# Doubling the angles of the S5 recurrence once for all groups of states, and a new order of the streams, in a two-layer mixer trunk

## Chip, cores and metric

One Trainium2 chip, one core. The metric is the device time of one execution in microseconds: 1331.64 us is the median of three runs of the kernel before (1329.62 to 1334.2 us).

## What is computed

A trunk of two layers over 512 tokens of width 1024, batch 1, all in float32. Each layer is

```python
h = rmsnorm(x, g)
for each branch n of (a, b, c, d, e):
    o_n = branch_n(h @ w_in)            # 256 columns
    mixed += sigmoid(h @ w_gate_n) * ((silu(h @ w_z_n) * o_n) @ w_out_n)
x = x + mixed @ w_out
```

with a: differential attention (two softmaxes per head, four heads in two pairs), b: dilated attention, c: an S5 state space recurrence, d: attention over compressed, selected and window keys, e: attention over a memory of 256 rows. The recurrence has 16 groups of channels, each with 64 complex states. Its transition over one step is a magnitude and an angle per state; the kernel works in chunks of 8 tokens (TC = 8) of which there are 64 (NJ = 64), so it needs cosine and sine of 8, 16, 32, ..., 256 times the angle of each state.

## The kernel before

**Products.** Every weight comes in halves of 128x512, in all 408. Each is split in a high part (`whi`, a ScalarE copy) and a low part (`wlo`), and every product takes three matmuls: high by high, low by high, high by low (`acc<-hh,whi`, `acc<-hl,whi`, `acc<-hh,wlo`). The low part is made in one of two ways, which `weights_hi` chooses for each half: by a VectorE subtraction (`wlo<-raw,whi`, 136 halves), or by a ScalarE copy with factor -1 and a GpSimd DMA that adds the weight from memory again (`wlo<-wu`, line 296, 272 halves).

**Streams.** The program is written as Python generators ("streams"): projections (each branch's q, k, v and the like from h), attentions (three workers that take the heads one by one), compression of branch d, recurrences, memories, and the trunk (gates and merges of the branches, 40 merge steps per layer, and the output product). While the program is built, a model of the engines runs with it: the stream with the lowest rank whose wake time has passed issues next. `RANK` (line 42) gives the ranks, `AFTER` (line 41) the event after which the recurrences (`s`, `c`) and memories begin, `PA` (line 44) how many heads of the branch before may still be unfinished when the next projections of d and a start. What the chip gets is the order that comes out, per engine; all instructions carry line 244 (line 286 for DMAs of SyncE's queue), so a group in the profile is told by its tiles.

**Names of tiles.** `acc`: a product's sum in PSUM; `sc`: scores; `prob`: probabilities (a ring of NPROB = 3); `pt`, `ph`, `pl`: a transposed tile and its high and low part; `o`: a head's output; `gate`: a merge's gate; `bl`, `bh`: the parts of a gated branch; `cxh`: inputs of the compression, whose products are `ms<-whi,cxh`; `tmp`: scratch; `u`, `uc`, `m`, `r`, `e`, `p`, `c`, `cs`: tiles of the recurrence; `s`: scratch of its parameters; `da`, `db`, `ck`, `sk`: four columns of an angle's doubling.

**Recurrence.** `s5_params` (from line 605) computes the parameters of all states of both layers at once, on tiles 128x16 (a column per layer and group of groups): exponentials, sine and cosine, and three doublings to 8 times the angle. `s5_table` (line 1550) makes, for each layer and each half of the groups, the table of 64 cosines and sines in six steps: six GpSimd products per step, and on VectorE ten operations on 128x4 tiles that double the angle, with a correction of its length, for the next step. Five such batches of ten belong to each of the four tables. `s5_operators` calls it and then `s5_powers`; `s5_in` makes `u`, sends it through memory (`ud`, `uc`) and `s5_chunks` does products with the states and a scan along the chunks (`r`). The recurrence of layer 0 runs beside its a heads and merges, that of layer 1 likewise.

**Heads of a.** `head_a` (line 1106) takes two probability tiles, one per softmax, and combines them.

## Time and profile before

| | before |
|---|---|
| time, median of three runs | 1331.64 us (1329.62 to 1334.2) |
| profiled execution | 1330.57 us |
| its span, first to last instruction | 1328.8 us |
| granted TensorE clock, mean | 0.984 |
| TensorE busy | 1261.2 us, 95% |
| VectorE busy | 917.0 us, 69% |
| ScalarE busy | 835.2 us, 63% |
| GpSimd busy | 433.8 us, 33% |
| data moved by DMA | 224.75 MB |

The span is the time from the first to the last instruction on the core; some 1.8 us of the execution lie outside it. In the trace's rows the first number is the start in microseconds from the span's start, the second the duration; matmuls overlap, so that two of 512 columns that last 0.39 us each start 0.23 us apart. In brackets stands how long the engine had been idle, and whose result ended that. Engines are named PE (TensorE), DVE (VectorE), ACT (ScalarE), POOL (GpSimd), SP (SyncE).

### The profile page before, as it was taken

Reading aid. Unit: us, or ns where it says so; the run is one execution under the profiler, and the core shown is the slowest. Engines: PE = TensorE matmul, PEld = TensorE weight load, DVE = VectorE, ACT = ScalarE, POOL = GpSimd, SP = SyncE. Lnnn points to the kernel's source line nnn. Section 1 sums busy time; section 2 is a strip of 40 time slices with the busy share of each in tenths; the row PEclk is TensorE's granted clock in tenths of the full one; section 3 lists DMA queues with packets and bytes.
Section 4 is the critical chain, followed back from the end, with each engine's and each line's share of the span. In section 5 each row is a group of like instructions: output and inputs, shape, how many; then the busy total and the mean of one; then the engine's idle time right before and its main releaser. Section 6 shows DMA issues by size and latency. Waiting matters only on the chain.

```text
span 1328.8 us, 19737 instructions
## 1 busy us (share of the span) xinstructions
PE 1261.2 (95%) x6303; PEld 1036.2 (78%) x6303; DVE 917.0 (69%) x2281; ACT 835.2 (63%) x1682; POOL 433.8 (33%) x551
## 2 busy tenths in 40 slices
PE   7699899999999999999989899999999999999996
PEld 4578678888887778888878588888877887888885
DVE  6879889667888775445338778677898776634542
ACT  6587877777774564655547767677768654455542
POOL 2643432221354262221223352122246335222112
PEclk9799999999999999999999899999999999999998
DMA  8484886754987788797766786374787888788751
GB/s 270 108 188 109 185 208 156 165 142 103 191 193 160 191 191 193 169 218 192 214 167 139 176 204 148 105 159 111 169 179 158 197 175 178 174 176 185 185 171 64
DMA packets 135816, 224.75 MB, mean 169 GB/s; under 512 B 23072, under 2 KB 30368, under 8 KB 135712
## 3 DMA queue, kind: packets, MB, share of 16 engines
q0 software_dynamic: 46080, 83.91, 38.8%
q1 hardware_dynamic: 89632, 139.59, 33.2%
q8 instruction: 49, 0.80, 0.2%
q14 instruction: 55, 0.45, 0.1%
HBM read 199.82 MB, written 23.56 MB: 168 GB/s over the span
## 4 chain that ended last, share of the span: by engine, by line
PE 74%; DVE 14%; DMA 5%; issue 3%; ACT 2%; POOL 1%; SPq 0%; DVEq 0%; POOLq 0%; ACTq 0%
PE acc L244 61%; PE ms L244 3%; PE sc L244 3%; PE o L244 3%; PE pt L244 3%; DVE prob L244 2%; DVE tmp L244 1%; DVE rope L244 1%; DMA raw<-wu 1%; DMA wlo<-wu 1%; DVE gate L244 1%; DVE c L244 1%; DVE pl L244 1%; POOL c L244 1%; POOL wlo L296 1%
## 5 line engine op out<-in xcount | busy, mean ns | idle before, releaser
L244 PE MATMUL acc<-hh,whi 128*128 128x512 f32 x1136 | 459.3, 404 | 10.8 <-ACT whi L244 6.2
L244 PE MATMUL acc<-hl,whi 128*128 128x512 f32 x1136 | 447.2, 394 | 1.3 <-DVE hl L244 1.3
L244 PE MATMUL acc<-hh,wlo 128*128 128x512 f32 x1136 | 446.9, 393 | 1.3 <-DVE wlo L244 1.3
L296 POOL DMA_DIRECT2D wlo<-wu x272 | 243.7, 913 | 606.2 <-ACT wlo L244 525.9
L244 ACT CAST whi<-raw 128x512 fp32r<-128x512 f32 x408 | 251.1, 617 | 265.4 <-PE acc L244 225.7
L244 PEld LDWEIGHTS acc<-hh,whi 128*128 128x128 f32 x1136 | 215.6, 190 | 58.6 <-issue 7.0
L244 PEld LDWEIGHTS acc<-hh,wlo 128*128 128x128 f32 x1136 | 215.1, 189 | 49.2 <-DVE wlo L244 2.2
L244 PEld LDWEIGHTS acc<-hl,whi 128*128 128x128 f32 x1136 | 216.0, 190 | 40.1 <-DVE hl L244 2.8
L244 ACT ACTIVATE wlo<-raw 128x512 fp32r<-128x512 f32 x272 | 170.2, 626 | 12.7 <-DMA raw<-wu 8.9
L244 DVE TENSOR_TENSOR wlo<-raw,whi 128x512 fp32r<-128x512 f32 x136 | 94.2, 696 | 45.7 <-ACT whi L244 45.4
L244 ACT ACTIVATE prob<-prob,nb 128x256 f32<-128x256 f32 (+3 forms) x160 | 89.3, 559 | 13.8 <-DVE nb L244 13.0
L244 ACT CAST ph<-pt 128x512 fp32r<-128x512 f32 (+1 forms) x112 | 58.2, 524 | 56.3 <-PE pt L244 53.7
L296 POOL DMA_DIRECT2D mixed<-gate x48 | 45.0, 937 | 140.2 <-DVE gate L244 98.7
L244 DVE TENSOR_TENSOR gate<-acc,rep 128x512 f32<-128x512 f32 x80 | 55.0, 688 | 49.4 <-PE acc L244 49.2
L244 DVE CUSTOM_DVE_ANT_0 prob<-sc,cst 128x128 f32<-128x128 f32 (+3 forms) x128 | 60.8, 486 | 31.7 <-PE sc L244 31.1
L244 PE MATMUL acc<-mx,whi 128*128 128x512 f32 (+1 forms) x288 | 81.0, 367 | 0.0
L244 DVE TENSOR_TENSOR pl<-pt,ph 128x512 fp32r<-128x512 f32 (+1 forms) x112 | 67.5, 608 | 18.6 <-ACT ph L244 18.3
L244 DVE SCALAR_TENSOR_TENSOR gate<-gate,acc 128x512 f32<-128x512 f32 x80 | 54.8, 685 | 28.1 <-ACT gate L244 23.8
L244 ACT ACTIVATE gate<-gate,hb 128x512 f32<-128x512 f32 x80 | 57.7, 721 | 15.4 <-DVE gate L244 15.2
L244 PE MATMUL pt<-cst,prob 128*128 128x128 f32 x384 | 61.9, 275 | 2.7 <-DVE prob L244 2.6
L244 PE MATMUL acc<-bh,whi 128*128 128x512 f32 x160 | 63.3, 396 | 0.8 <-DVE gate L244 0.8
L244 PE MATMUL acc<-bl,whi 128*128 128x512 f32 x160 | 62.6, 392 | 1.0 <-DVE bl L244 1.0
(310 smaller groups left out, 2110.4 us busy)
## 6 DMA issues: line engine op xcount, KB each, us to landing
raw<-wu SPq DMA_DIRECT2D x408, 256.0 KB, 4.3
wlo<-wu POOLq DMA_DIRECT2D x272, 256.0 KB, 5.6
mixed<-gate POOLq DMA_DIRECT2D x48, 256.0 KB, 5.0
mixed<-gate SPq DMA_DIRECT2D x16, 256.0 KB, 4.8
gate<-mixed SPq DMA_DIRECT2D x16, 256.0 KB, 4.3
x<-xT SPq DMA_DIRECT2D x8, 256.0 KB, 5.8
tab<-rope SPq DMA_DIRECT2D x8, 256.0 KB, 6.5
mraw<-memT SPq DMA_DIRECT2D x8, 256.0 KB, 5.8
```

The lines of the kernel that those rows point to most:

```text
L244: getattr(self.eng, name)(out, *args, **kw)
L296: self.eng.dma_start(out, src, accum_op=ALU.add)
```

## The change

1. `s5_params` goes on doubling, from 8 to 256 times the angle, on its 128x16 tiles, and keeps the six cosines and sines. These are five more rounds of ten VectorE operations, once. `s5_table` reads them: its five batches of ten operations on 128x4 tiles, for each of four tables, are gone (200 VectorE operations less, 50 more). The GpSimd products stay.
2. `AFTER['s']` is `pb` in place of `mem`: the parameters may begin after layer 0's projections of b, not after the memories'.
3. The attentions' rank is 4, not 3.
4. `PA[1]` is 1, not 4: in layer 0 the projections of a's second pair wait until at most one head of the first pair is left.
5. `head_a` waits until fewer than NPROB - 1 = 2 others hold a pair of probability tiles.

```diff
--- before.py
+++ after.py
@@ -38,10 +38,10 @@
 LAT = 100
 ORDER = ('beda', 'edba')
 MERGES = ('bedac', 'edbac')
-AFTER = {'s': 'mem', 'c': ('mem', 'ob'), 'm': ('b', 'a')}
-RANK = {'att': 3, 'cmp': 1, 'rec': 2, 'ch': 6, 'proj': 4, 'trunk': 5, 'mem': 3}
+AFTER = {'s': 'pb', 'c': ('mem', 'ob'), 'm': ('b', 'a')}
+RANK = {'att': 4, 'cmp': 1, 'rec': 2, 'ch': 6, 'proj': 4, 'trunk': 5, 'mem': 3}
 WORKERS = 3
-PA = (4, 4, 2, 1)
+PA = (4, 1, 2, 1)
 MEM0 = ('rep', 0)
 
 MAGIC = 12582912.0
@@ -599,7 +599,7 @@
 
     C16 = 16
     s5p = {}
-    for n in ("mag8", "c8", "s8", "zr", "zi", "ar1", "ai1", "ar2", "ai2", "ar4", "ai4"):
+    for n in (*(f"{x}{TC << i}" for x in "cs" for i in range(6)), "mag8", "zr", "zi", "ar1", "ai1", "ar2", "ai2", "ar4", "ai4"):
         s5p[n] = cp.tile([128, C16], F32, name="s5" + n)
 
     def s5_params():
@@ -687,23 +687,28 @@
         v.tensor_mul(zi, zi, den)
 
         c, s, m = cs, sn, mag
-        for n in (2, 4, 8):
-            c2, s2, m2 = (s5p["c8"], s5p["s8"], s5p["mag8"]) if n == 8 else (t16("c"), t16("s"), t16("m"))
+        n = 1
+        while n < TC * NJ // 2:
+            n *= 2
+            c2, s2 = (s5p[f"c{n}"], s5p[f"s{n}"]) if n >= TC else (t16("c"), t16("s"))
             v.tensor_mul(c2, c, c)
             v.tensor_mul(t, s, s)
             v.tensor_sub(c2, c2, t)
             v.scalar_tensor_tensor(s2, c, 2.0, s, ALU.mult, ALU.mult)
-            v.tensor_mul(m2, m, m)
+            if n <= TC:
+                m2 = s5p["mag8"] if n == TC else t16("m")
+                v.tensor_mul(m2, m, m)
+                m = m2
             v.tensor_mul(t, c2, c2)
             v.tensor_mul(u, s2, s2)
             v.tensor_add(t, t, u)
             v.tensor_scalar(t, t, -0.5, 1.5, ALU.mult, ALU.add)
             v.tensor_mul(c2, c2, t)
             v.tensor_mul(s2, s2, t)
-            if n < 8:
+            if n < TC:
                 v.tensor_mul(s5p[f"ar{n}"], m2, c2)
                 v.tensor_mul(s5p[f"ai{n}"], m2, s2)
-            c, s, m = c2, s2, m2
+            c, s = c2, s2
         for eng, name, args in ops:
             getattr(eng, name)(*args)
             yield eng.now + 130
@@ -1089,7 +1094,7 @@
         R["pa", l, i] = st, vs
 
 
-    outs, left = {}, {}
+    outs, left, pairs = {}, {}, []
 
     def out_tile(key):
         if key not in outs:
@@ -1108,6 +1113,8 @@
         st, vs = R["pa", l, i]
         vv = [x.rearrange("p (t h c) -> p t h c", t=2, h=2) for x in vs]
         ps, ds = [], []
+        yield lambda: len(pairs) < NPROB - 1
+        pairs.append(0)
         for c in range(2):
             q, k = st["a_q", hh], st["a_k", hh]
 
@@ -1117,6 +1124,7 @@
             p, den = yield from causal_exp(qk, causal, SC32)
             ps.append(p)
             ds.append(den)
+        pairs.pop()
         free(st["a_q", hh], st["a_k", hh])
         r0, r1 = recip(ds[0], 4), recip(ds[1], 4)
         V.tensor_scalar(r1[:, :4], r1[:, :4], lam[l], None, ALU.mult)
@@ -1553,9 +1561,9 @@
         V.memset(ct[:, :, 0:1], 1.0)
         V.memset(st[:, :, 0:1], 0.0)
         o = 8 * l + 4 * h
-        ck, sk = s5p["c8"][:, o:o + 4], s5p["s8"][:, o:o + 4]
         n = 1
         while n < NJ:
+            ck, sk = s5p[f"c{TC * n}"][:, o:o + 4], s5p[f"s{TC * n}"][:, o:o + 4]
             x, y = (xy[:, 128 * i:128 * i + 128].rearrange("p (s t) -> p s t", s=4)[:, :, 0:n] for i in range(2))
             cb, sb = ck.unsqueeze(2).to_broadcast([128, 4, n]), sk.unsqueeze(2).to_broadcast([128, 4, n])
             c0, s0 = ct[:, :, 0:n], st[:, :, 0:n]
@@ -1568,19 +1576,6 @@
             G.tensor_tensor(y, c0, sb, ALU.mult)
             G.tensor_tensor(s1, x, y, ALU.add)
             n *= 2
-            if n < NJ:
-                a, b, c, s = small(4, "da"), small(4, "db"), small(4, "ck"), small(4, "sk")
-                V.tensor_mul(a, ck, ck)
-                V.tensor_mul(b, sk, sk)
-                V.tensor_sub(c, a, b)
-                V.scalar_tensor_tensor(s, ck, 2.0, sk, ALU.mult, ALU.mult)
-                V.tensor_mul(a, c, c)
-                V.tensor_mul(b, s, s)
-                V.tensor_add(a, a, b)
-                V.tensor_scalar(a, a, -0.5, 1.5, ALU.mult, ALU.add)
-                V.tensor_mul(c, c, a)
-                V.tensor_mul(s, s, a)
-                ck, sk = c, s
 
     def s5_powers(l, h, x, y, tmp, conj):
```

Edits 2 to 5 and the missing operations change the order that comes out. TensorE's instructions are the same ones. VectorE has 2119 in place of 2259, among them 146 low parts in place of 136; ScalarE makes 262 low parts in place of 272, and GpSimd issues as many accumulating DMAs fewer. Up to the 270th row of TensorE (about 79 us of the trace of before), from about 555 to 1005 us and from about 1195 us the orders of all engines are alike. Between, in layer 0, the value projections of d (dv) come after the compression, the projections of a's second pair move from among the merges to right behind layer 0's silu projection of d, and the first `u` with them; the recurrence's second `u` and its output come at other merges. In layer 1 the first `u` comes one merge earlier, and the second one too.

The first place is VectorE in layer 1, where the second table of the recurrence is made while the merges run. `gate` with `acc,rep` is a merge's gate, `da`, `db`, `ck`, `sk` are a batch, `u` is the input of the second half. Before:

```order
L244 TENSOR_TENSOR sk_12187<-sk_12187,da_12184 128x4
L244 TENSOR_TENSOR da_12224<-ck_12186 128x4
L244 TENSOR_TENSOR db_12225<-sk_12187 128x4
L244 TENSOR_TENSOR ck_12226<-da_12224,db_12225 128x4
L244 SCALAR_TENSOR_TENSOR sk_12227<-ck_12186,sk_12187 128x4
L244 TENSOR_TENSOR da_12224<-ck_12226 128x4
L244 TENSOR_TENSOR db_12225<-sk_12227 128x4
L244 TENSOR_TENSOR da_12224<-da_12224,db_12225 128x4
L244 TENSOR_SCALAR da_12224<-da_12224 128x4
L244 TENSOR_TENSOR ck_12226<-ck_12226,da_12224 128x4
L244 TENSOR_TENSOR sk_12227<-sk_12227,da_12224 128x4
L244 TENSOR_TENSOR gate_12245<-acc_12165,rep_7521 128x512
```

The change:

```order
L244 TENSOR_TENSOR gate_12021<-acc_11907,rep_7434 128x512
L244 TENSOR_TENSOR wlo_11930<-raw_11847,whi_11982 128x512
L244 TENSOR_TENSOR wlo_11984<-raw_11878,whi_12030 128x512
L244 SCALAR_TENSOR_TENSOR gate_12021<-gate_12021,acc_12023 128x512
L244 TENSOR_TENSOR wlo_12057<-raw_11937,whi_12083 128x512
L244 TENSOR_TENSOR u_12104<-acc_12070,rep_7434 128x512
L244 TENSOR_TENSOR wlo_12085<-raw_12042,whi_12101 128x512
```

Between a gate and the operation ahead of it stood twenty operations of the doubling, the last eleven of them shown; now the gate follows the `cs` set-up, and low parts follow it.

The second place is TensorE in layer 0, around the compression. `o<-ph,vm` and `pt<-cst,prob` belong to heads of the memory branch, `ms<-whi,cxh` to the compression. Before, `acc_1499` is the product dv:

```order
L244 MATMUL acc_1499<-hh_106,whi_1241 128x512
L244 MATMUL acc_1499<-hl_114,whi_1241 128x512
L244 MATMUL acc_1499<-hh_106,wlo_1206 128x512
L244 MATMUL o_1424<-ph_1473,vm_724 128x512
L244 MATMUL o_1424<-pl_1474,vm_724 128x512
L244 MATMUL pt_1574<-cst,prob_1167 128x128 x4
L244 MATMUL acc_1594<-hh_99,whi_1292 128x512
L244 MATMUL acc_1594<-hl_107,whi_1292 128x512
L244 MATMUL acc_1594<-hh_99,wlo_1244 128x512
L244 MATMUL acc_1594<-hh_100,whi_1292 128x512
L244 MATMUL acc_1594<-hl_108,whi_1292 128x512
L244 MATMUL acc_1594<-hh_100,wlo_1244 128x512
```

The change, where `acc_1521` is another product of which half is done:

```order
L244 MATMUL acc_1521<-hh_112,wlo_1117 128x512
L244 MATMUL sc_1554<-kms_593,eq_1034 128x256
L244 MATMUL sc_1554<-kml_595,eq_1034 128x256
L244 MATMUL sc_1554<-kms_593,eq_1034 128x256
L244 MATMUL sc_1554<-kml_595,eq_1034 128x256
L244 MATMUL o_1437<-ph_1486,vm_734 128x512
L244 MATMUL o_1437<-pl_1487,vm_734 128x512
L244 MATMUL pt_1577<-cst,prob_1180 128x128 x4
L244 MATMUL pt_1589<-cst,prob_1389 128x128 x4
L244 MATMUL ms_1611<-whi_1254,cxh_1502 64x256
L244 MATMUL ms_1611<-wlo_1219,cxh_1502 32x256 x2
L244 MATMUL ms_1611<-whi_1254,cxh_1502 64x256
```

The 24 matmuls of dv stood ahead of these rows, and matmuls of the next product behind `pt`; now the score, the value products, two transposes and the compression follow one another, and dv comes after the compression.

The third place is VectorE in layer 0, where the second pair of a's heads is taken up. `prob<-sc` (printed as ISA) is a score's maximum, `rec` and `prob<-prob,rec` the scaling of the finished probabilities, `r` the recurrence's scan chain. Before:

```order
L244 TENSOR_TENSOR ck_4643<-ck_4643,da_4641 128x4
L244 TENSOR_TENSOR sk_4644<-sk_4644,da_4641 128x4
L244 TENSOR_SCALAR rec_4655<-den_4269 128x4
L244 RECIPROCAL rec_4655<-rec_4655 128x4
L244 TENSOR_SCALAR rec_4658<-den_4463 128x4
L244 RECIPROCAL rec_4658<-rec_4658 128x4
L244 TENSOR_SCALAR rec_4658<-rec_4658,lam_3045 128x4
L244 TENSOR_SCALAR prob_4461<-prob_4461,rec_4658 128x128
L244 SCALAR_TENSOR_TENSOR prob_4267<-prob_4267,rec_4655,prob_4461 128x128
L244 TENSOR_SCALAR prob_4461<-prob_4461,rec_4658 128x256
L244 SCALAR_TENSOR_TENSOR prob_4267<-prob_4267,rec_4655,prob_4461 128x256
L244 TENSOR_SCALAR prob_4461<-prob_4461,rec_4658 128x384
```

The change:

```order
L244 ISA prob_4576,nb_4577<-sc_4644,cst 128x512
L244 ISA nb_4577 128x1
L244 ISA prob_4582,nb_4583<-sc_4650,cst 128x512
L244 ISA nb_4583 128x1
L244 TENSOR_TENSOR r_4508<-ms_4653,cs_4317 128x256
L244 TENSOR_TENSOR r_4509<-ms_4653,cs_4317 128x256 x2
L244 TENSOR_TENSOR r_4508<-ms_4653,cs_4317 128x256
L244 TENSOR_TENSOR r_4508<-r_4508,r_4509 128x256
L244 SCALAR_TENSOR_TENSOR r_4508<-cs_4318,r_4508 128x256
L244 TENSOR_TENSOR r_4508<-r_4508,r_4509 128x256
L244 SCALAR_TENSOR_TENSOR r_4508<-cs_4318,r_4508 128x256
L244 SCALAR_TENSOR_TENSOR tmp_4636<-tmp_4636,tmp_4637 128x512
```

Ahead of the scaling stood the end of a batch; the scores of two heads now stand alternately, and the first chunk's scan chain is right behind them.

## Rows read from the trace of the kernel before

**Rows 1.** The page: busy shares, the chain, and two groups of VectorE (busy us, mean ns).

```profile
PE 1261.2 (95%) x6303; PEld 1036.2 (78%) x6303; DVE 917.0 (69%) x2281; ACT 835.2 (63%) x1682; POOL 433.8 (33%) x551
...
PE 74%; DVE 14%; DMA 5%; issue 3%; ACT 2%; POOL 1%; SPq 0%; DVEq 0%; POOLq 0%; ACTq 0%
...
L244 DVE TENSOR_TENSOR wlo<-raw,whi 128x512 fp32r<-128x512 f32 x136 | 94.2, 696 | 45.7 <-ACT whi L244 45.4
...
L244 DVE CUSTOM_DVE_ANT_0 prob<-sc,cst 128x128 f32<-128x128 f32 (+3 forms) x128 | 60.8, 486 | 31.7 <-PE sc L244 31.1
```

**Rows 2.** Windows of the changed stretches: from:to, length, each engine's busy us, clock, DMA share.

```profile
79.00:200.00 121.00, 113.10 (x595) 91.25 (x594) 106.46 (x281) 95.16 (x213) 47.15 (x44) 1.00 0.74 171
200.00:400.00 200.00, 199.11 (x1000) 166.09 (x999) 158.24 (x495) 146.94 (x322) 62.98 (x91) 1.00 0.71 157
400.00:555.00 155.00, 148.55 (x811) 122.50 (x810) 105.02 (x268) 83.97 (x151) 55.97 (x86) 1.00 0.81 182
...
1005.00:1195.00 190.00, 186.01 (x936) 151.65 (x935) 124.19 (x352) 107.76 (x197) 74.58 (x126) 1.00 0.80 176
```

**Rows 3.** Timeline of TensorE, layer 0: start, length, operation, idle before and its releaser.

```profile
144.30 0.66 PE L244 MATMUL acc<-cst,tmp 128*128 128x128 f32 x4 [3.18 <-DVE tmp L244]
...
150.94 0.30 PE L244 MATMUL ms<-wlo,cxh 128*32 128x256 f32 x1 [0.86 <-DMA wlo<-wu]
...
184.40 0.50 PE L244 MATMUL acc<-bl,whi 128*128 128x512 f32 x1 [0.53 <-DVE bl L244]
...
401.53 0.33 PE L244 MATMUL pt<-cst,prob 128*128 128x128 f32 x1 [0.71 <-DVE prob L244]
402.88 0.33 PE L244 MATMUL pt<-cst,prob 128*128 128x128 f32 x1 [1.02 <-DVE prob L244]
...
406.00 0.50 PE L244 MATMUL o<-pl,vs 128*128 128x512 f32 x1 [0.95 <-DVE pl L244]
...
413.02 1.15 PE L244 MATMUL ms<-uc,m 128*64 128x64 f32 x32 [0.53 <-DMA uc<-ud]
...
471.94 0.47 PE L244 MATMUL acc<-hh,whi 128*128 128x512 f32 x1 [1.91 <-DVE gate L244]
```

**Rows 4.** The same in layer 1.

```profile
1012.40 0.50 PE L244 MATMUL acc<-bh,whi 128*128 128x512 f32 x1 [0.78 <-DVE gate L244]
...
1121.58 0.50 PE L244 MATMUL acc<-hh,whi 128*128 128x512 f32 x1 [1.70 <-DVE gate L244]
...
1144.54 0.43 PE L244 MATMUL ms<-r,e 128*128 128x63 f32 x2 [0.80 <-DVE r L244]
```

**Rows 5.** Timeline of VectorE before the gate that the matmul at 1121.58 waited for.

```profile
1118.06 0.15 DVE L244 TENSOR_TENSOR da<-ck 128x4 f32<-128x4 f32 x1
...
1120.85 0.68 DVE L244 TENSOR_TENSOR gate<-acc,rep 128x512 f32<-128x512 f32 x1
```

**Rows 6.** VectorE's operations by line and shape, 84 to 254 us.

```profile
L244 DVE TENSOR_TENSOR s<-s 128x16 f32<-128x16 f32 x40 | 9.8, 247 | 0.2
```

**Rows 7.** Timeline of TensorE, the window's products at the compression.

```profile
136.83 0.40 PE L244 MATMUL o<-ph,vm 128*128 128x512 f32 x1
137.06 0.39 PE L244 MATMUL o<-pl,vm 128*128 128x512 f32 x1
```

**Rows 8.** Timeline of VectorE, then of GpSimd, in the same place.

```profile
136.10 0.68 DVE L244 TENSOR_TENSOR pl<-pt,ph 128x512 fp32r<-128x512 f32 x1
...
140.15 1.50 DVE L244 TENSOR_TENSOR cxh<-xa,cxh 128x256 fp32r<-128x256 f32 x1
...
145.00 0.43 DVE L244 TENSOR_TENSOR cxh<-xa,cxh 128x256 fp32r<-128x256 f32 x1
...
139.75 1.63 POOL L244 TENSOR_TENSOR rope<-rope,tab 128x512 f32<-128x512 f32 x1 [0.45 <-DVE rope L244]
```

**Rows 9.** Timeline of VectorE, the scan chain of layer 1's second chunk: its ends.

```profile
1138.03 1.42 DVE L244 TENSOR_TENSOR r<-ms,cs 128x256 f32<-128x256 f32 x4 [2.19 <-PE ms L244]
...
1143.63 1.75 DVE L244 TENSOR_TENSOR r<-r,r 64x256 f32<-64x256 f32 x4
```

## Prediction

> **What bounds the kernel now.** I read the page's busy shares and chain first. TensorE is busy for 1261.2 of 1328.8 us and makes up 74% of the chain that ended last [rows 1]; the reader should see that no other engine can set the end for long, so that the time changes only where TensorE stands still: 67.6 us in all. The profiled execution took 1330.57 us, 1.07 us below the median of 1331.64; the sum below is made against 1330.57.
>
> Next I compared the order of the instructions before and after, engine by engine. Up to about 79 us, from 555 to 1005 us and from 1195 us to the end the two orders are the same row by row, on every engine; only 79 to 555 us (layer 0) and 1005 to 1195 us (layer 1) differ, and TensorE's matmuls are the same ones. So I cut the trace at these times. In the four changed stretches TensorE is idle for 121.00 - 113.10 = 7.9, 0.9, 155.00 - 148.55 = 6.45 and 4.0 us, 19.2 us together, which bounds what can be won; from 200 to 400 us there is nothing to win [rows 2]. VectorE is at 106.46 of 121 us in the first of them, nearest to being a bound itself.
>
> Third, the timeline of TensorE in these stretches, for the waits one by one and who ends them: nearly all end on a VectorE result [rows 3, 4]. What VectorE does in front of that result is then the question.
>
> **The change, part by part.**
>
> *Doublings.* Layer 1 loses 100 VectorE instructions on 128x4 tiles, layer 0 loses 100 of them and gains 50 on 128x16. In the piece with two batches of ten, 20 of the small ones take 1118.06 to 1120.85, 2.79 us or 0.14 us each [rows 5]. So 100 are worth 14 us of VectorE. A 128x16 operation of the parameter stream took 0.247 us on average [rows 6]; 50 are 12.4 us. Ten halves of weights get their low part by a VectorE subtraction in place of a ScalarE operation and an accumulating DMA, seven of them in layer 0: 7 x 0.696 = 4.9 us [rows 1]. Layer 0 therefore wins nothing on VectorE (14.0 - 12.4 - 4.9 = -3.3 us) but gets the doublings early, in the stretch where TensorE hardly waits, in place of in front of heads and merges; layer 1 wins 14.0 - 3 x 0.696 = 11.9 us. ScalarE and GpSimd lose ten instructions each, and the GpSimd queue ten DMAs of 256 KB; neither engine ends one of the waits listed, so I put that at nothing; a DMA ended one of them (0.86 us, [rows 3]), which bounds it.
>
> *Where that reaches TensorE, layer 1.* The wait of 1.70 us at 1121.58 is for a gate that starts at 1120.85, right behind the 20 small operations [rows 4, 5]. Its sum of matmuls had ended before them, so with them gone it starts up to 2.79 us earlier: **-1.7**. The wait of 0.78 at 1012.40 has a batch ahead as well, but its gate began as soon as its own accumulation was done; between 0 and -0.78 I take **-0.5**. The wait of 0.80 at 1144.54 is for the scan chain, which starts earlier in the new order and has more matmuls between its parts: **-0.8**, 0 at worst.
>
> *Layer 0, from 400 us.* The three waits at 401.53, 402.88 and 406.00 (2.68 us) are for the probabilities of a head that stand on VectorE behind table batches and a merge's operations [rows 3]. In the new order these batches are gone and the heads stand elsewhere: **-2.7**. The 0.53 us at 413.02 is for the channel data on their way through memory; u is now computed some hundred matmuls earlier and its transfers with it: **-0.5**. The 1.91 us at 471.94 is for a gate behind a row of the state powers' products; in the new order that gate and those products are apart: **-1.9**, with 0 as the other end, since the products must go somewhere. Together the waits that go are 1.7 + 0.5 + 0.8 + 2.7 + 0.5 + 1.9 = 8.1 us.
>
> *What comes in their place, first place: compression (about 134 to 150 us).* The d branch's value product dv stood as cover between the window's scores and the compression's products; now it comes after them. Its 24 matmuls, which start 0.23 us apart [rows 7], cover 5.5 us. VectorE's order up to there is unchanged, so I walk along it. Before, TensorE waited 3.18 and 0.86 us here [rows 3]. The product with ph and pl, which began at 136.83 [rows 7], is now reached twelve matmuls earlier, at 136.83 - 12 x 0.23 = 134.1, and its half with pl at 134.3; but pl ends at 136.78 [rows 8]: 2.4 us of wait. Then come the next probabilities (0.6), the first compressed input cxh (1.0), the second (0.8), then pl of two heads behind four rotated results (2.2 and 0.5): 7.5 us in all. That is 3.5 more than the 4.04 before. But the 5.5 us of dv are still to be done and cover later waits of this stretch, where VectorE must catch up; the 0.53 us at 184.40 [rows 3] is one of them. I give back half: **+1.7**. Bounds: +3.5 if nothing is given back, -3.2 if the queue in front of cxh clears and most of the old waits go.
>
> Here a rule speaks. The second input took VectorE 0.43 us, the first one 1.50 us, while GpSimd ran a rotation product of 1.63 us that had started 0.39 us before [rows 8]. The Trainium skill (SBUF — State Buffer, Who interferes with whom) says that a VectorE instruction with two SBUF inputs and a GpSimd instruction that reads SBUF hold one port pair in turn, whoever starts first, for the whole instruction. The trace agrees (1.50 against 0.43 us). In the new order the first input stands ahead of the rotation's shuffle and the second one behind it, so it is again one of them that is held: the sum keeps the 1.07 us. By the rule, should VectorE be first, they would go, and the sum would be 1.1 us better.
>
> *Second place: two heads and the scan chain (before about 400 us).* The new order takes up the two heads of the second pair together and puts the first chunk of the recurrence right behind them. Between the heads' first scores and the first product with r, VectorE has eight score operations (8 x 0.486 = 3.9 us [rows 1]), four half-merges and a normalization (some 4 us at 0.69 each), one more score, and a scan chain that took 1138.03 to 1145.38, 7.35 us with one operation of another stream in it [rows 9]: 15 to 15.6 us. TensorE has 36 matmuls of 512 columns, 36 x 0.23 = 8.3 us [rows 7], and about 2 us of scores and small products: 10.3. But the starts on VectorE lie closer than the durations, by about an eighth in these rows, which makes 13.5; and part of the scores lie where TensorE is already ahead. I take **+1.5**; ends 0 (the scores done beforehand) and +5.3 (no cover).
>
> *Third place: layer 1's first chunk* now meets three heads. By the same count VectorE has twelve scores, the scan chain and eight operations of 0.69 us, 5.8 + 7.35 + 5.5 = 18.7 us, beside 69 matmuls of 0.23, 15.9 us, and the small ones: **+1.0**, 0 to +2.6.
>
> *The other edits* (the second pair's projections wait for one head, a bound on heads that hold probabilities) show only through the order, which is counted above.
>
> Sum: -8.1 + 1.7 + 1.5 + 1.0 = -3.9 us; 1330.57 - 3.9 = **1326.7 us**.
>
> **The rivals.**
>
> *Slower: the VectorE queue at the three places.* Mechanism: work that was spread stands in one row on VectorE, TensorE has no matmul left to put in between. Price at the full ends: 3.5 + 5.3 + 2.6 = 11.4 us of new waits. Against it stand the 8.1 us, of which 1.9 (products moved) may stay: 11.4 - 6.2 = +5.2, 1335.8 us. For it: VectorE at 106.46 of 121 us [rows 2], and that dv is taken away as cover where the longest wait (3.18) already was. Against it: in 200 to 400 us VectorE has 158.24 of 200 us and TensorE lost nothing. It decides when TensorE's new idle time at the three places passes 8 us.
>
> *No net change: waits move only.* The total of VectorE in layer 0 is the same within 3.3 us, so its 7.9 and 6.45 us of idle time stay, wherever; of the gain only layer 1's firm part, 1.7 us, is left: 1328.9 us. This is also what comes out if the change does what it says and nearly all of it lay beside matmuls anyway.
>
> *More: no wait takes the place of the old ones.* The 8.1 us and the two old waits at the compression (4.04) go: 1330.6 - 12.1 = 1318.5 us. For it: an order in which VectorE's small work lies in the quiet stretch; against it the walk above, where pl ends late by the old row's time.
>
> **How the numbers follow.** A difference of under 0.3%, 4 us, cannot be told from none. Chances: forecast 0.42, with its own range 1323 to 1329 (0.32 of it beyond 0.3%, 0.10 within); more 0.15; moved only 0.22; slower 0.21. Faster 0.32 + 0.15 = 0.47, same 0.10 + 0.22 = 0.32, slower 0.21. The range runs from the rival "more" less the 1.07 us by which the first input was the longer, and a margin of 1.5 us for the DMA waits I left alone, 1316, to the slower rival, 1336; what is left out is the outer half of both, about 2 in 10.
>
> **What would show it.** Right: TensorE's busy time unchanged at 1261 us; no wait over 0.5 us at the counterparts of 1121.58 and of 401 to 406 us; from 555 to 1005 us the same length within a microsecond; new waits on pl and cxh at the compression of 5 to 8 us, on r in layer 0 of 1 to 3. Wrong: a layer 0 stretch that is longer than 476 us, a wait for r or a head's score of more than 5 us in one piece, a granted clock below 1.00 in the changed stretches (it is 1.00 in all four [rows 2]), or idle time that comes back in 1195 us to the end.

## The result, and the profile after

The change is slower: 1341.26 us, median of eight runs (1337.79 to 1346.41), beside 1334.08 us of the kernel before on the same chip; the ratio is 1.0064, 95% interval 1.0047 to 1.0081. The forecast was 1326.7 us, and the range ended at 1336. The profiled execution took 1340.22 us, its span is 1338.4 us, the mean granted clock 0.980 (before 0.984).

The page of the changed kernel, the lines that answer to [rows 1], and the row of the granted clock in 40 slices:

```profile
PE 1268.4 (95%) x6303; PEld 1042.8 (78%) x6303; DVE 903.2 (67%) x2141; ACT 830.6 (62%) x1672; POOL 424.2 (32%) x541
...
PEclk9799899999998999999999999999999999999998
...
PE 79%; DVE 9%; issue 4%; DMA 3%; POOL 2%; ACT 2%; SPq 0%; DVEq 0%; POOLq 0%; ACTq 0%
...
L244 DVE TENSOR_TENSOR wlo<-raw,whi 128x512 fp32r<-128x512 f32 x146 | 102.8, 706 | 61.1 <-ACT whi L244 60.8
```

VectorE did become 13.8 us shorter, and its share of the chain fell from 14% to 9%. But TensorE is busy 7.2 us longer with the same 6303 matmuls, and that points to the clock.

Next the windows. The first three answer to [rows 2]; the next three cut the program at the same matmuls as the windows of before below them (layer 0's changed stretch, the unchanged one, layer 1's).

```profile
79.00:200.00 121.00, 111.20 (x577) 90.25 (x576) 103.97 (x280) 87.91 (x200) 40.74 (x37) 0.97 0.66 151
200.00:400.00 200.00, 193.94 (x971) 161.08 (x970) 152.87 (x466) 136.89 (x292) 63.19 (x90) 0.99 0.67 152
400.00:560.00 160.00, 155.85 (x829) 129.40 (x828) 106.56 (x255) 97.32 (x190) 56.19 (x88) 0.97 0.83 186
...
80.10:566.50 486.40, 466.40 (x2393) 385.06 (x2393) 365.19 (x997) 323.49 (x681) 160.10 (x214) 0.98 0.72 163
...
566.50:1019.30 452.80, 436.60 (x2123) 357.79 (x2122) 311.62 (x691) 294.60 (x609) 132.43 (x139) 0.99 0.70 166
...
1019.30:1187.90 168.60, 166.17 (x852) 136.34 (x852) 106.02 (x244) 97.81 (x181) 65.82 (x117) 1.00 0.76 168
```

The kernel before, cut at the same matmuls:

```profile
78.90:552.50 473.60, 458.36 (x2392) 377.88 (x2391) 368.64 (x1040) 323.88 (x683) 166.10 (x219) 1.00 0.75 170
...
552.50:1006.20 453.70, 439.64 (x2123) 360.70 (x2122) 310.94 (x698) 297.92 (x616) 132.95 (x140) 0.98 0.70 167
...
1006.20:1177.30 171.10, 167.11 (x851) 136.01 (x850) 116.52 (x334) 97.64 (x181) 70.19 (x121) 1.00 0.82 178
```

Layer 0 is 486.40 - 473.60 = 12.8 us longer: TensorE's idle time grew from 15.2 to 20.0 us (+4.8), and the same matmuls took 466.40 in place of 458.36 us (+8.0), at a mean clock of 0.98 in place of 1.00. The stretch between is 0.9 us shorter and layer 1 2.5 us; the start is 1.2 us longer and the end 1.0 us shorter. So the loss is in layer 0, and TensorE's busy time grew there more than its waits did.

The waits of TensorE there, which answer to [rows 3]:

```profile
138.31 0.50 PE L244 MATMUL o<-pl,vm 128*128 128x512 f32 x1 [2.35 <-DVE pl L244]
...
141.88 0.47 PE L244 MATMUL ms<-whi,cxh 128*64 128x256 f32 x1 [1.90 <-ACT prob L244]
...
192.23 0.30 PE L244 MATMUL ms<-wlo,cxh 128*32 128x256 f32 x1 [1.55 <-DMA wlo<-wu]
...
225.30 0.47 PE L244 MATMUL acc<-hh,whi 128*128 128x512 f32 x1 [2.73 <-DVE s L244]
...
376.56 0.44 PE L244 MATMUL o<-pl,vs 128*128 128x384 f32 x1 [1.89 <-DVE pl L244]
...
398.52 0.66 PE L244 MATMUL acc<-cst,tmp 128*128 128x128 f32 x4 [1.43 <-DVE tmp L244]
...
405.30 0.51 PE L244 MATMUL acc<-hh,wlo 128*128 128x512 f32 x1 [1.10 <-DMA wlo<-wu]
...
419.65 0.43 PE L244 MATMUL ms<-r,e 128*128 128x63 f32 x2 [1.84 <-DVE r L244]
```

The three waits of [rows 3] at 401 to 406 us and the one at 471.94 have no counterpart any more. The wait of 2.35 us for pl and that for r are as the prediction walked them. Those at 225.30, 376.56 and 398.52, and those for a DMA at 192.23 and 405.30, it did not have.

Three windows, each inside a stretch in which every clock record is the lower one, and two matmuls of the last of them:

```profile
140.40:147.00 6.60, 5.12 (x24) 4.60 (x25) 6.47 (x11) 5.89 (x14) 5.46 (x6) 0.50 0.35 62
225.80:229.00 3.20, 3.20 (x9) 2.33 (x9) 2.98 (x12) 0.72 (x1) 0.00 (x0) 0.50 0.73 141
420.30:430.30 10.00, 9.77 (x37) 8.99 (x37) 3.24 (x9) 2.46 (x6) 0.00 (x0) 0.50 0.60 131
```

```profile
427.85 0.63 PE L244 MATMUL acc<-bh,whi 128*128 128x512 f32 x1
428.27 0.63 PE L244 MATMUL acc<-bl,whi 128*128 128x512 f32 x1
```

At these places the chip granted 1.2 in place of 2.4 GHz: 0.50. Such a stretch is called a drop below. The first begins at 140.3 us, behind the wait of 2.35 us and inside that of 1.90, the others behind the waits of 2.73 and 1.84 us. There matmuls of 512 columns start 0.42 us apart in place of 0.23 [rows 7]. With their edges the drops are 6.8, 3.4 and 10.2 us long, 20.4 together; in layer 0 the kernel before had none. Half of that, 10.2 us, is the most that can be lost; TensorE's busy time grew by 8.0. The Trainium skill (TensorE: Matmul & The Clock Gate, HAM oscillation — how this bites in real kernels) also counts half of the time at the lower clock as lost. Here that is an upper end: what the drops cost in time is 5.6 us, as the runs with fill show below.

### The profile page after: what moved, and what is told of

Read it like the earlier page. It is cut to its first block, busy times and chain, and to the rows that moved or that the text cites. A ratio compares the mean times of both kernels' runs of the same rounds, so it can differ in the third digit from the quotient of the medians.

```text
span 1338.4 us, 19563 instructions
## 1 busy us (share of the span) xinstructions
PE 1268.4 (95%) x6303; PEld 1042.8 (78%) x6303; DVE 903.2 (67%) x2141; ACT 830.6 (62%) x1672; POOL 424.2 (32%) x541
## 4 chain that ended last, share of the span: by engine, by line
PE 79%; DVE 9%; issue 4%; DMA 3%; POOL 2%; ACT 2%; SPq 0%; DVEq 0%; POOLq 0%; ACTq 0%
PE acc L244 67%; PE ms L244 3%; PE sc L244 3%; PE o L244 3%; PE pt L244 3%; DMA wlo<-wu 2%; DVE c L244 1%; DVE rope L244 1%; POOL c L244 1%; DVE tmp L244 1%; DVE p L244 1%; POOL cs L244 1%; DMA raw<-wu 1%; DVE r L244 0%; DVE prob L244 0%
## 5 line engine op out<-in xcount | busy, mean ns | idle before, releaser
L296 POOL DMA_DIRECT2D wlo<-wu x262 | 234.7, 911 | 641.8 <-ACT wlo L244 524.7
L244 ACT ACTIVATE wlo<-raw 128x512 fp32r<-128x512 f32 x262 | 164.1, 626 | 14.9 <-DMA raw<-wu 12.6
L244 DVE TENSOR_TENSOR wlo<-raw,whi 128x512 fp32r<-128x512 f32 x146 | 102.8, 706 | 61.1 <-ACT whi L244 60.8
L244 ACT ACTIVATE prob<-prob,nb 128x256 f32<-128x256 f32 (+3 forms) x160 | 89.2, 559 | 19.2 <-DVE nb L244 18.4
L244 DVE TENSOR_TENSOR gate<-acc,rep 128x512 f32<-128x512 f32 x80 | 55.1, 688 | 64.5 <-PE acc L244 64.2
L244 ACT ACTIVATE gate<-gate,hb 128x512 f32<-128x512 f32 x80 | 57.7, 721 | 12.8 <-DVE gate L244 12.7
L244 PE MATMUL acc<-bh,wlo 128*128 128x512 f32 x160 | 62.8, 393 | 0.0
```

The lines of the kernel that those rows point to most:

```text
L244: getattr(self.eng, name)(out, *args, **kw)
L296: self.eng.dma_start(out, src, accum_op=ALU.add)
```

## Experiments

Three causes stood against each other: the **clock** (Theory A: the half clock behind the waits costs as well as the waits), the **order** (Rival W: its waits as such, whatever the clock does), and the **doublings** (Rival D: 50 operations on 128x16 tiles more in layer 0). Theory O of the last three runs says that the doublings by themselves are worth what the prediction counted, and that the loss comes from the order. Ratios are to the kernel before on the same chip. "Fill" is a run of matmuls whose sums are overwritten by the next product in their PSUM tile; it is left out of the model of the engines, so that the order stays as it is.

### e2_constants: the new constants without the moved doublings

```diff
-AFTER = {'s': 'mem', 'c': ('mem', 'ob'), 'm': ('b', 'a')}
-RANK = {'att': 3, 'cmp': 1, 'rec': 2, 'ch': 6, 'proj': 4, 'trunk': 5, 'mem': 3}
+AFTER = {'s': 'pb', 'c': ('mem', 'ob'), 'm': ('b', 'a')}
+RANK = {'att': 4, 'cmp': 1, 'rec': 2, 'ch': 6, 'proj': 4, 'trunk': 5, 'mem': 3}
...
-PA = (4, 4, 2, 1)
+PA = (4, 1, 2, 1)
...
+        yield lambda: len(pairs) < NPROB - 1
```

> The new constants of the order alone, doublings on 128x4 tiles as before (TensorE's order at the compression is the changed kernel's, layer 1's is that of before). Theory A: the waits at the compression and the half clock behind them are there, +5 to +8 us, and layer 1 wins nothing; ratio 1.003 to 1.009. Rival D: as before, 0.998 to 1.002.

1359.63 us, ratio 1.0210 (1.0188 to 1.0232), far above both forecasts. A wait of it, and a window of the half clock around it:

```profile
307.73 1.22 PE L244 MATMUL o<-ch,vc 128*128 128x512 f32 x2 [4.79 <-DVE o L244]
```

```profile
305.00:313.00 8.00, 5.27 (x23) 4.83 (x23) 6.90 (x19) 2.79 (x7) 2.02 (x7) 0.57 0.42 85
```

At least seven stretches of layer 0 are at half clock here. The new constants alone lose more than the whole change does: an order that is this slow comes out without the moved doublings too.

### f_a and f_ac: fill at the compression, and at the first scan chain too

Both are the change with the first of these edits, ahead of the compression's first product; f_ac has the second one too, ahead of the products that the first scan chain feeds.

```diff
             ps = yield from take("ms")
+            if l == 0 and kv == 0:
+                fill(ps, 0, 8)
...
         ps = yield from take("ms")
+        if l == 0 and h == 0:
+            fill(ps, 0, 8)
```

> The changed kernel with eight matmuls of 512 columns put where TensorE stood idle for 1.90 us ahead of the compression's first product in layer 0 (their sums are overwritten; every other instruction is in the same order). Theory A: TensorE has work in the wait, the half clock from 140.3 to 147.1 us does not come, and the 27 short products behind take 0.114 us each, not 0.213: 3 us less than the changed kernel, ratio 1.003 to 1.005. Rival W (the waits are the whole loss and the clock is only their company): the fill replaces idle time and nothing else changes, 1.006 to 1.007; if it delays the products, 1.007 to 1.008.

> As f_a, and eight more such matmuls ahead of the first scan chain's products in layer 0, where TensorE waited 1.84 us for r and its clock was half from 420.2 to 430.4 us. Theory A: the second half-clock stretch goes as well, another 4 to 5 us: 7 to 8 us less than the changed kernel, ratio 1.000 to 1.002. Rival W: 1.006 to 1.008.

f_a 1345.68 us, ratio 1.0102 (1.0082 to 1.0122), above both forecasts; f_ac 1339.36 us, 1.0053 (1.0032 to 1.0073), between the two. The fill of f_a:

```profile
142.39 3.78 PE L1691 MATMUL ms<-hh 128*128 128x512 f32 x8 [1.88 <-ACT prob L244]
```

It stands behind the wait, not in it: the clock had already fallen, and its eight matmuls ran at half speed, 3.78 us. It only cost. At the scan chain the fill did its work: f_ac differs from f_a by that fill alone, was timed on the same chip, and is 6.3 us faster, with intervals that lie apart. Where it comes from is read in f_c (next but one).

### e1b_doublings: the moved doublings with the old constants

> The doublings alone, with AFTER, RANK and PA as before, and with the bound on heads that hold probabilities kept. TensorE's order is that of before up to about 240 us (compression and first merges included), layer 1's is the changed kernel's. Theory A (the loss sits where the new constants leave TensorE short of work in layer 0, in waits and in the half clock that follows them): no half clock at 140 and 225 us, layer 1 gains 2.6 us; ratio 0.996 to 1.001. Rival D (the 50 operations on 128x16 tiles cost): 1.005 to 1.008. The first scan chain of layer 0 is the open place: with a half-clock stretch there, up to 1.004.

1343.12 us, ratio 1.0092 (1.0058 to 1.0126), the median above both forecasts. The bound on heads stays in: without it (e1_doublings) two heads can each hold a probability tile and wait for a second one, no stream can go on while the program is put together, and there is no kernel and no time. Its longest wait, and the window around it:

```profile
474.22 1.08 PE L244 MATMUL pt<-cst,p 128*128 128x128 f32 x4 [4.89 <-DVE p L244]
```

```profile
465.00:480.00 15.00, 7.29 (x26) 5.12 (x27) 11.38 (x32) 5.57 (x13) 3.49 (x10) 0.54 0.54 142
```

So the doublings alone are slow too, but as soon as they are moved the model of the engines puts out yet another order, here with the powers' products piled up. Doublings and order are not apart in this run; that needed same_order.

### v_after_mem, f_c, f_abc

v_after_mem is the change without edit 2:

```diff
-AFTER = {'s': 'pb', 'c': ('mem', 'ob'), 'm': ('b', 'a')}
+AFTER = {'s': 'mem', 'c': ('mem', 'ob'), 'm': ('b', 'a')}
```

f_c is the change with the second fill of f_ac alone. f_abc adds to f_c ten matmuls ahead of the wait for pl at the compression and twelve ahead of the wait at 225 us:

```diff
+            if (l, h, kt) == (0, 0, 0) and T.eng is not None:
+                for _ in range(10):
+                    T.eng.matmul(o, vm[kt][:, h, :], ph, start=True, stop=True)
...
+            if (l, n, m) == (0, 1, 2) and T.eng is not None:
+                for _ in range(12):
+                    T.eng.matmul(y, wb[0][:, m % 2, 0, :], bps[0][0], start=True, stop=True)
```

> The changed kernel with AFTER['s'] back at mem and the rest of its constants. The order is that of before at the compression (with dv ahead of it), the changed kernel's in layer 1. Theory A: the waits and the half clock at 140 us go, 3 to 6 us less than the changed kernel there; the scan chain of layer 0 with its half clock may stay; ratio 0.998 to 1.004. Rival (the loss is spread over all waits of layer 0 in proportion to VectorE's work, which is the same): 1.005 to 1.008.

> The changed kernel with the eight matmuls ahead of the first scan chain's products in layer 0 alone. The profile with both fills showed 4.6 us less there and no half clock, and nothing won at the compression, where the clock had fallen before the fill came. Theory A: 4 to 5 us less than the changed kernel, ratio 1.002 to 1.004. Rival W (that profile was a lucky one, the waits are the loss): 1.006 to 1.008.

> The changed kernel with fills at three places of layer 0: ten matmuls in the wait for pl ahead of the compression (where the first 2.35 us of idle time lie, ahead of the fall of the clock), twelve in the wait for the gate at 225 us (2.73 us), eight at the first scan chain. Theory A: none of the three half-clock stretches (140 to 147, 226 to 229, 420 to 430 us) is left: 3 + 1.5 + 4.6 = 9 us less than the changed kernel; ratio 0.999 to 1.001. Rival W: 1.005 to 1.009.

v_after_mem 1339.01 us, ratio 1.0045 (1.0022 to 1.0067): it lies between the two forecasts and its interval meets that of the change, so edit 2 is not told apart as a cause; its drops in layer 0 are elsewhere (221.9, 368.7, 505.2 us). What edits 3 to 5 cost one by one was not run.

f_c 1337.64 us, ratio 1.0029 (1.0011 to 1.0048), inside what the clock theory gave. A window of f_c, its fill, and the first product with r:

```profile
417.00:431.00 14.00, 13.77 (x76) 11.77 (x76) 10.54 (x28) 6.22 (x14) 3.17 (x4) 1.00 0.84 186
...
415.45 2.00 PE L1689 MATMUL ms<-hh 128*128 128x512 f32 x8
...
417.62 0.43 PE L244 MATMUL ms<-r,e 128*128 128x63 f32 x2
```

The drop at 420 us is gone: TensorE starts 76 matmuls in these 14 us, at a clock of 1.00. Against the changed kernel, row by row, f_c is 2.0 us ahead before the fill, 0.2 behind it, and 2.0 again at the first product with r: the eight matmuls took just what the wait of 1.84 us gave back. At 431 us f_c is 6.6 us ahead, and so it is at the end of layer 0. So this drop costs 4.6 us; f_ac and f_abc, row by row, give 4.6 too. The eight useless matmuls win back about half of the loss (1.0064 to 1.0029; the two intervals just meet). This shows the clock as a cause, with a size. In f_c's profile the drop at 225 us did not come either, though nothing was put there; from 225 to 229 us it gains 1.0 us on the changed kernel, which is the price of that drop.

f_abc 1339.8 us, ratio 1.0044 (1.0024 to 1.0063); the clock theory had expected it at 0.999 to 1.001, Rival W at 1.005 or more: a miss of both. The three old drops are gone. But at the first of these places nothing was won. The stretch of the drop, and the product with pl behind it:

```profile
140.00:147.00 7.00, 3.67 (x29) 3.25 (x29) 6.84 (x9) 6.30 (x14) 6.39 (x6) 1.00 0.51 110
...
147.18 0.50 PE L244 MATMUL o<-pl,vm 128*128 128x512 f32 x1 [2.55 <-DVE pl L244]
```

With the clock at 1.00 TensorE is done with the compression's products 2.4 us earlier against the changed kernel, and then waits 2.55 us for pl, which VectorE makes no sooner. The changed kernel begins this product at 148.06 without a wait; f_abc was 0.92 us ahead behind its first fill and is 0.88 ahead here. So the drop at 140 us cost no time: it stood in place of a wait. At 225 us f_abc gains 1.0 us, as f_c does. And two other drops came:

```profile
149.00:157.00 8.00, 6.64 (x23) 5.68 (x24) 6.55 (x18) 3.76 (x10) 0.00 (x0) 0.57 0.83 172
...
378.00:382.00 4.00, 4.00 (x17) 3.37 (x16) 3.80 (x11) 2.55 (x6) 0.12 (x1) 0.57 1.02 243
```

The second comes behind the 1.9 us wait for pl that the changed kernel has as well (376.56), and where its clock held. The 30 matmuls cost up to 30 x 0.23 = 6.9 us, where they don't fill a wait. In this execution, taking three drops away was followed by two others.

### same_order, extra50, same_fill: the order held

same_order is the kernel before with the doublings moved as in the change, but every other instruction in its old place on every engine: the model of the engines still counts the old operations, which aren't issued, and the 50 new ones go behind every third VectorE instruction from about 254 us on. extra50 adds those 50 without taking any away, their results unused. same_fill is same_order with two fills in layer 1, nine matmuls ahead of the memory scores and eight ahead of branch d's gate transposes. The first part is in all three, the last two in same_fill:

```diff
+                if self.later:
+                    self.turn += 1
+                    if self.turn % 3 == 0:
+                        op, a = self.later.pop(0)
+                        getattr(self.eng, op)(*a)
...
+            if (l, h, g) == (1, 0, 0):
+                fill(s, 1, 9)
...
+        if l == 1:
+            fill(pt, 1, 8)
```

> The doublings moved and nothing else: all engines in the order of the kernel before, row by row, less the 200 operations on 128x4 tiles, with the 50 on 128x16 put behind every third VectorE instruction from about 254 us. The low parts of the weights are made as before. Theory O (the doublings by themselves are worth what the prediction counted, and the loss comes from the new order): the waits of 1.70 us at 1121 us and of 2.7 us at 401 to 406 us go, TensorE loses nothing in 254 to 330 us; 3 to 6 us faster than before, ratio 0.995 to 0.999. Rival D (the operations on 128x16 tiles cost more than they save): 1.001 to 1.006.

> The kernel before with the 50 operations on 128x16 tiles added at the same places and nothing taken away (their results are not used). Theory O: they lie beside matmuls in a stretch where TensorE lost nothing; ratio 0.999 to 1.002, some 8 to 14 us more VectorE time. Rival D: 1.003 or more.

> As same_order, with matmuls of 512 columns put in two waits of layer 1 behind which the clock was half in the profile of before: nine in the wait of 2.26 us ahead of the first memory scores (697 us; half clock 698.9 to 702.3) and eight in that of 2.12 us ahead of the gates' transposes in branch d (753 us; half clock 753.5 to 760.3). Their sums are overwritten. Theory A (idle time of TensorE of this length brings the clock down, and the matmuls behind it then take twice as long): 1.7 and 3 us less than same_order, ratio 0.992 to 0.996. Rival W (the clock falls there for other reasons, or the fill comes too late): as same_order or up to 2 us more.

same_order 1333.35 us, ratio 1.0003 (0.9987 to 1.0020): no change, where 0.995 to 0.999 was expected. extra50 1333.35 us, 0.9993 (0.9978 to 1.0007). So the 50 operations cost nothing that can be told apart, and doublings that don't change the order win at most 1.7 us, the lower end of the interval, though VectorE is busy 19.2 us less (897.8 us). In same_order the wait at 1121.58 is gone, as the prediction had it. But in extra50, which keeps the twenty small operations there, most of it is gone too:

```profile
1121.93 0.50 PE L245 MATMUL acc<-hh,whi 128*128 128x512 f32 x1 [0.35 <-DVE gate L245]
```

TensorE came there 1.7 us later than in the profile of before, and the gate only 0.34 us later: a wait that is gone can be one that TensorE was too late for. Of the waits at 401 to 406 us half is gone, and the transfer behind waits longer, 1.43 us where it was 0.53 [rows 3]:

```profile
403.69 0.33 PE L245 MATMUL pt<-cst,prob 128*128 128x128 f32 x1 [0.42 <-DVE prob L245]
...
406.92 0.50 PE L245 MATMUL o<-pl,vs 128*128 128x512 f32 x1 [0.92 <-DVE pl L245]
...
414.85 1.15 PE L245 MATMUL ms<-uc,m 128*64 128x64 f32 x32 [1.43 <-DMA uc<-ud]
```

Row by row, same_order is level with before at 1146 us (0.02 us behind) and 3.3 us behind it at 1154 us. The same window of same_order, then of before:

```profile
1146.00:1155.00 9.00, 9.00 (x38) 7.85 (x38) 2.80 (x5) 1.83 (x3) 0.87 (x1) 0.62 0.53 127
```

```profile
1146.00:1155.00 9.00, 9.00 (x52) 7.86 (x52) 3.46 (x6) 2.34 (x4) 0.87 (x1) 1.00 0.54 121
```

extra50 has 0.62 there too, and same_fill 0.51 from 1143 to 1150 us, where it reaches the same rows. All four wait 0.80 and 0.23 us for r just ahead: the same order and the same waits, with the clock fallen in three executions of four. It cost 3.2 us in each of the three.

same_fill 1332.73 us, 0.9997 (0.9982 to 1.0011), where 0.992 to 0.996 was expected: a miss, and the time that Rival W gave. The profile has the two drops gone that before has at 699 and 753 us; its windows there:

```profile
695.00:705.00 10.00, 8.60 (x45) 6.67 (x44) 8.01 (x16) 7.54 (x23) 0.00 (x0) 1.00 0.27 79
752.00:762.00 10.00, 8.57 (x50) 6.06 (x48) 6.18 (x20) 6.23 (x14) 2.58 (x3) 1.00 1.06 250
```

Row by row against before this won 0.5 us behind 699 us, where a wait for a probability tile grew from 0.43 to 1.19 us, and 2.6 us behind 753 us, of which 1.6 went by 764 us into waits. And over its 12 runs the time at half clock fell only from 49.5 to 45.5 us against same_order, of which half is 2 us, and the 17 matmuls cost part of that.

### All runs together

The time at half clock of a run is 2 x (1 - mean clock) x span. Means over all runs (those of before are from two chips):

| kernel | runs | time, us | at half clock, us | time less half of that |
|---|---|---|---|---|
| before | 71 | 1333.4 | 49.8 | 1308.5 |
| the change | 8 | 1341.4 | 64.3 | 1309.3 |
| e2_constants | 5 | 1360.4 | 78.3 | 1321.3 |
| e1b_doublings | 8 | 1344.7 | 64.5 | 1312.4 |
| f_a / f_ac | 6 / 6 | 1346.0 / 1338.4 | 66.8 / 53.9 | 1312.6 / 1311.4 |
| f_c / f_abc | 12 / 12 | 1337.1 / 1339.1 | 54.3 / 50.4 | 1309.9 / 1314.0 |
| v_after_mem | 12 | 1339.3 | 57.1 | 1310.7 |
| same_order / same_fill | 12 / 12 | 1333.8 / 1333.3 | 49.5 / 45.5 | 1309.1 / 1310.5 |
| extra50 | 12 | 1333.0 | 47.3 | 1309.4 |

The change is 8.0 us slower on average and spends 14.5 us more at half clock; half of that is 7.2 us, and with it taken off the two kernels are within 0.8 us of each other. But half is the upper end. By what the three drops of layer 0 cost (5.6 of 20.4 us) it is 4 us, by the spread of the kernel before (0.34 us per us, last section) 5 us. So by this estimate 4 to 7 of the 8 us go with the clock, and the rest is waits. The last column is worked out, not measured: no run of the changed order without drops was found. No kernel here is told apart from before as faster.

## Why the prediction was wrong

**The clock.** The step that failed is the sum itself: it prices every wait at its own length, and takes the clock of 1.00 of [rows 2] over into the new order. The prediction named a clock below 1.00 only as a sign that it was wrong, without a price. None of the rivals had it. It put 8.0 us more busy time into layer 0. The runs with fill price its three drops at 0, 1.0 and 4.6 us, together 5.6 us: some 2.4 us of the busy time stood in place of a wait for pl. The rest of the 12.8 us that layer 0 grew, 7.2 us, is waits, where the sum had -1.9: it put the stretch from 200 to 400 us and the DMAs of the low parts at nothing, and that is the second step that failed.

**The waits of layer 0** were to sum to -2.7 - 0.5 - 1.9 + 1.7 + 1.5 = -1.9 us; they came to +4.8 as read off the rows:

| place | forecast | measured |
|---|---|---|
| compression, 134 to 193 us | +1.7 | +1.7 (6.1 to 7.8; of it DMA 1.1 to 3.6) |
| 401 to 413 us | -3.2 | -3.2 |
| wait for r | +1.5 | +2.1 |
| gate at 471.94 | -1.9 | -1.9, and +1.9 at 376.56 |
| 225.30 and 398.52 | none | +2.3 and +1.4 |
| DMA at 405.30 | none | +1.1 |
| the rest, each under 0.9 | none | -0.6 |

The scan chain came out well. At the compression the +1.7 agrees by luck. The walk had 7.5 us of waits: 2.4 for pl came (2.35), 2.4 for probabilities and inputs came as 1.90, and 2.7 for pl of two heads did not come, because the products ahead of them ran at half clock; in f_abc, where they did not, it is 2.55. In their place came waits for the weights' low parts by DMA. In all of layer 0 these grew from 1.95 to 4.65 us, a term that the prediction had put at nothing. The gate of 471.94 is the step for which 0 was named as the other end, "since the products must go somewhere": they did. VectorE of the changed kernel ahead of the ends of the waits at 225.30 and 376.56, where `vs` and `s`, and pl, stand behind what was moved:

```profile
221.88 2.82 DVE L244 TENSOR_TENSOR dst<-rope,dst 32x512 fp32r<-32x512 f32 x4
224.73 0.42 DVE L244 TENSOR_TENSOR vs<-acc,vs 128x256 fp32r<-128x256 f32 x1
225.07 0.17 DVE L244 TENSOR_TENSOR s<-s 128x16 f32<-128x16 f32 x1
225.15 0.68 DVE L244 TENSOR_TENSOR gate<-acc,rep 128x512 f32<-128x512 f32 x1
...
371.06 1.41 DVE L244 TENSOR_TENSOR c<-p,s5ar 128x128 f32<-128x128 f32 x1
...
375.82 0.68 DVE L244 TENSOR_TENSOR pl<-pt,ph 128x512 fp32r<-128x512 f32 x1
```

At 225 us (the gate ends at 225.83, so it did not end that wait) it is the rotated results of a's second pair, 2.82 us in one row; from 371 to 376 us the powers' products; at 398.52 rotated results again. From 200 to 400 us the prediction had said that there was nothing to win, and did not ask what there was to lose: these three waits, 6.05 us, are all of TensorE's idle time there (200.00 - 193.94).

**Layer 1** was to give -1.7 - 0.5 - 0.8 + 1.0 = -2.0 us and gave -2.5, of which 1.6 in waits. The waits at 1121.58 and 1144.54 are gone; that of 0.78 at 1012.40 stayed, and the third place cost 1.62:

```profile
1025.53 0.50 PE L244 MATMUL acc<-hh,whi 128*128 128x512 f32 x1 [0.79 <-DVE gate L244]
...
1034.63 1.02 PE L244 MATMUL ms<-cst,tmp 128*128 128x2 f32 x8 [1.62 <-DVE nb L244]
```

**The rivals.** "The VectorE queue at three places" had the right sign but not the cause: the new waits there are 1.7 + 2.1 + 1.6 = 5.4 us, under the 8 from which it decides. Its mechanism did occur, at other places: 225.30, 376.56 and 398.52. "Moved only" is what same_order shows of the doublings by themselves: 1.0003.

**The port.** At the compression the sum kept 1.07 us, because one of the two inputs would again be held up by GpSimd's rotation [rows 8]. VectorE, then GpSimd of the changed kernel there:

```profile
140.31 0.42 DVE L244 TENSOR_TENSOR cxh<-xa,cxh 128x256 fp32r<-128x256 f32 x1
...
141.86 1.25 DVE L244 TENSOR_SCALAR s<-s 128x16 f32<-128x16 f32 x1
143.03 0.41 DVE L244 TENSOR_TENSOR cxh<-xa,cxh 128x256 fp32r<-128x256 f32 x1
...
141.46 1.62 POOL L244 TENSOR_TENSOR rope<-rope,tab 128x512 f32<-128x512 f32 x1 [4.55 <-DVE rope L244]
```

Both inputs now took 0.41 us, but a small operation of the parameters, which elsewhere take 0.17 us (the one at 225.07 above), took 1.25 us in front of the second, while the rotation ran. So about the 1.07 us stayed, but by luck: neither input was held, another operation was. Before, such an operation was held in front of the second input as well (1.23 us at 141.58).

## What to carry to other kernels

On a kernel whose TensorE is 95% busy, the price of a new order is not the sum of its waits: give the half clock that may follow a new wait a term and a rival of its own. Price a drop by the rows behind it: here one of 6.8 us cost nothing, because the next wait took it up, and one of 10.2 us cost 4.6. When a change makes a planner put out a new order, hold the order once and make the edit alone: here one such run showed that the saved operations were worth 1.7 us at most. Work that leaves one row of a queue stands in another: here it made new waits in a stretch that had been quiet.

## What was not expected of the hardware

**A fallen clock can't be read from the length of the wait ahead of it.** The clock held behind 3.18 us in the kernel before [rows 3] and behind 1.89 us in the changed one; it fell behind 2.73 and 1.84 us, and behind 1.90 us in f_abc. Behind the same wait of 2.73 us it held in f_c.

**It differs between executions of one order.** At 1146 us it fell in same_order, extra50 and same_fill and not in before, behind the same waits. Over the 71 runs of before the time at half clock goes from 37 to 64 us, and the device time goes with it (correlation 0.84), by 0.34 us for each us at half clock: most of the spread of this kernel's times goes with its clock. Why one execution falls and the next does not stays open.

**A drop costs only what no later wait takes up.** At 420 us 10.2 us cost 4.6 and at 1146 us 6.8 cost 3.2, with TensorE busy nearly throughout; at 140 us 6.8 cost nothing, as 2.55 us of waiting for VectorE would have stood there. So TensorE's busy time overstates the price: in layer 0 it grew by 8.0 us, where the drops cost 5.6.
